# Fewer early weight sums beside the embedding, and the spread of the value differences from another engine's DMA queue

## The chip, the core and the metric

The kernel runs on one core of one Trainium2 chip. The metric is the device time of one execution in microseconds (us). The kernel before takes 813.34 us, the median of three runs (813.11 to 813.79).

## The reference

One layer of a small trunk, in float32, for 512 positions of width 2048. With depth 1 only the first mixer runs, sliding-window attention:

```
hn = rmsnorm(x, norm_g)
q, k, v, gate = split(hn @ swa_w_in)         # 32 query heads, 4 key/value heads, 64 wide
scores = q k^T / 8 + bias(distance), masked to a window of 128 back
probs  = softmax with a sink term in the denominator
y   = (probs v * silu(gate)) @ swa_w_out
x   = x + y
emb = p @ ple_proj                           # 512 x 256 @ 256 x 2048
g   = sigmoid(rmsnorm(x, ple_norm) @ ple_gate)
out = rmsnorm(x + emb * g, final_g)
```

## The kernel before

TensorE multiplies float32 as three products of a high and a low part (`mm3`, L129 to L134): ScalarE casts each block of weights to its high part (`whi`, L115), VectorE subtracts to get the low part (`wlo`, L116), and three matmuls of 512 columns follow. A block of weights is 128 x 1024 floats, 512 KB. `Weights` (L88) loads them through SyncE's queue (L105) into three raw buffers; a raw buffer is free again when the `wlo` of three blocks before is made.

The program has four stretches: the first products of q, k and v while x streams in (to about 71 us), the first gate block (71 to 81 us), the **embedding** `emb = p @ ple_proj` (`embed`, L903; 81.5 to 103.3 us on TensorE), and the attention loop (L944), in which TensorE's long projections (`proj`) are interleaved with 64 small attention blocks. After it come the output projection and the gate of the embedding, both as Strassen-like seven products of sub-blocks. Those need sums of blocks of weights (`w_out`, `ple_gate`), and the sums are prepared in DRAM long before: `sum_weights(i)` (L697) issues on even steps a copy of one block, DRAM to DRAM, from SyncE's queue (L700), and on odd steps, seven steps behind, an accumulating DMA onto that copy from GpSimd's queue (L702). There are 118 steps (`SUM_STEPS`), of which the first `SUMS_EARLY` belong to the embedding and the rest are spread evenly over the 64 attention blocks (`sums_in`, L932).

The embedding has 16 small steps (j = 0 to 3 over columns, t = 0 to 3 over rows), each with six matmuls into a bank of PSUM. For even t ScalarE copies the bank out (L914), for odd t VectorE does (L916), and GpSimd's queue then stores the pair to DRAM (`embedded`, L917). The copies go to a tile with three buffers (tag `u`), so the copy for one pair waits until the store of the third pair before it has landed. At t = 1 of each j the next block of weights is loaded, cast and subtracted (L919). Beside it run "chores" (L452): GpSimd builds differences of neighbouring value tiles (L441, L442), ScalarE and VectorE split them in high and low parts (L386, L387), and `spread_diff` (L446) copies them within SBUF to the places where the attention reads them (`DV`, first read by L595). That is four DMAs of 64 rows x 2 KB for each of three differences, twelve in all, and they are issued from SyncE's queue. In the order of the 16 steps (n = 4j + t) the three spreads come at n = 7, 9 and 11; the loads of weights come at n = 1, 5, 9 and 13, after the matmuls and ahead of the chores of the same step. The sums come last in a step.

Here the order of TensorE, SyncE, VectorE, ScalarE and GpSimd is the order of the program (`manual_schedule`, L351). Every engine runs its instructions in that order, and an instruction that waits holds up what stands behind it on its engine, DMA issues included.

The blocks of weights are numbered as they are loaded: 0 and 1 are the first gate block, 2 is `p` transposed, 3 to 6 are `ple_proj`, 7 and 8 the first block of q in the attention loop, 9 and 10 the second. "raw 8" below is the load of block 8, "whi 8" and "wlo 8" its parts.

Of the kernel before, what the change touches and what calls it, by code (L numbers as in the profile page):

```python
# [11 lines left out]
F32 = mybir.dt.float32  # L12
# [17 lines left out]
HB = P // 2  # L30
# [25 lines left out]
def trunk_kernel(ctx: ExitStack, tc: tile.TileContext, a: dict):  # L56
    nc = tc.nc
# [151 lines left out]
    for k in range(KC):  # L209
# [54 lines left out]
        else:  # L264
            high()
            if k == 1:
                src = xw[:, w_at[512] : w_at[512] + 256]
# [143 lines left out]
    for b in range(exact, BUCKETS):  # L411
        d = np.nonzero(bk == b)[0]
        if len(d):
            lo, n = P - 1 + int(d.min()), len(d)
# [16 lines left out]
    DV = apool.tile([P, NB - 1, 2, KVH * 2 * HD], F32R, name="DV")  # L431
# [14 lines left out]
    def spread_diff(n):  # L446
        src = diffs["all"][:, (n - 1) * S : n * S]
        for b in range(2):
            for o in range(2):
                nc.sync.dma_start(DV[HB * o : HB * o + HB, n - 1, b].bitcast(F32), src[HB * b : HB * b + HB])  # L450

    def first_chores(i, step):  # L452

        if step == 0 and i < NB - 1:
            make_diff(i + 1)
        if step and 1 <= i < NB:
            diffs[i][step - 1]()
        if step == 2 and 1 <= i - 1 < NB:
            spread_diff(i - 1)
        if step and 1 <= i - 2 < NB:  # L460
            split(V[i - 2], values[i - 2])[step - 1]()
# [230 lines left out]
                copies.append((t, block(nm, *first, jj, m) if first else summed[nm, {6: 7, 4: 6}[p], jj, m]))  # L692
                adds.append((t, block(nm, *{7: (2, 2), 5: (1, 2), 6: (1, 1), 4: (2, 1)}[p], jj, m)))
    SUM_STEPS = 2 * len(copies) + 6
    SUMS_EARLY = 16

    def sum_weights(i):  # L697

# [204 lines left out]
    def embed():  # L903

        h, l = (v.rearrange("p k c -> p (k c)").rearrange("p (k t) -> p k t", k=2) for v in W.get(2))
        for j in range(4):
            wh, wl = (v.rearrange("p k c -> p (k c)").rearrange("p (k c) -> p k c", k=2) for v in W.get(3 + j))
            for t in range(NB):
                e_ps = bank(f"e{t}_{j}", "to"[t % 2])
                for k in range(2):  # L910
                    mm3(e_ps, h[:, k, blk(t)], l[:, k, blk(t)], wh[:, k], wl[:, k], k == 0, k == 1)
                if t % 2 == 0:
                    both = apool.tile([P, 2, S], F32, tag="u", name=f"both{t}_{j}", bufs=3)
                    nc.scalar.copy(both[:, 0], e_ps)  # L914
                else:
                    nc.vector.tensor_copy(both[:, 1], e_ps)  # L916
                    nc.gpsimd.dma_start(embedded[t // 2, j], both.rearrange("p b c -> p (b c)"))  # L917
                if t == 1 and W.todo:
                    W.todo.pop(0)()  # L919
                for _ in range(2 if t == 3 else 1):  # L920
                    first_chores(*next(early_chores, (NB + 2, 0)))
                for n in early_sums.get(4 * j + t, ()):
                    sum_weights(n)
        for v in early_chores:
            first_chores(*v)

    early_chores = ((i, step) for i in range(NB + 2) for step in range(3))
    early_sums = {0: range(0, 4, 2), 2: range(4, 8, 2), 4: range(8, 12, 2), 6: range(12, 16, 2), 8: (7, 9), 11: (11, 13), 14: (15,)}
    embed()
    blocks = TWOS * UNITS  # L930

    def sums_in(i):  # L932

        n = SUM_STEPS - SUMS_EARLY
        return range(SUMS_EARLY + i * n // blocks, SUMS_EARLY + (i + 1) * n // blocks)

# [464 lines left out]
    n = done[3]  # L1401
# [87 lines left out]
```

## Time and profile before

| | |
|---|---|
| median of three runs | 813.34 us |
| profiled execution | 813.76 us |
| its span, first to last instruction | 812.1 us |
| TensorE busy | 786.7 us (97%) |
| VectorE busy | 585.3 us (72%) |
| ScalarE busy | 506.8 us (62%) |
| GpSimd busy | 148.7 us (18%) |
| moved by DMA | 191.52 MB, mean 236 GB/s |
| SyncE's DMA queue (q1, hardware) | 52.6% of 16 DMA engines' span |
| GpSimd's DMA queue (q0, software) | 28.1% |

PE is TensorE, PEld its weight loads, DVE is VectorE, ACT is ScalarE, POOL is GpSimd, SP is SyncE; SPq is SyncE's queue issuing a DMA. A row of the timeline has start, duration, engine, line, operation, tiles and count, and in brackets the idle time before it and what ended it. A row of waits has the total, the number and the longest. PEclk is the granted clock of TensorE as a share of full speed. "DMA share" is the mean busy share of the 16 DMA engines. Matmuls overlap, so their starts are counted here and not their durations.

### The profile page before, as it was taken

The numbers are of one execution on the slowest core, as the hardware profiler recorded it, in microseconds if no ns is written. First come the engines' busy times: TensorE is split into PE (matmuls) and PEld (weight loads), VectorE is DVE, ScalarE is ACT, GpSimd is POOL, SyncE is SP. The second block draws the span as 40 slices with busy tenths as digits, with TensorE's granted clock in tenths as the row PEclk, the third lists the DMA queues.
The fourth block names the chain that finished last, engine by engine and source line by source line (L and its number), as shares of the span: only waits on it lengthen the run. The fifth ranks groups of instructions, "written<-read, shape, count | busy, mean of one in ns | idle before, by whom it ended". The sixth has DMA issues, their size and how long they took to land.

```text
span 812.1 us, 11213 instructions
## 1 busy us (share of the span) xinstructions
PE 786.7 (97%) x3740; PEld 655.6 (81%) x3740; DVE 585.3 (72%) x1159; ACT 506.8 (62%) x1071; POOL 148.7 (18%) x256
## 2 busy tenths in 40 slices
PE   9999959999999999999999999999999999999993
PEld 8888838888888888888888888888888888888883
DVE  4555426877587767867676779977887675798986
ACT  6652425867576666766665665445668865666855
POOL 0200420323233141323233310000000012030100
PEclk9999979999999999999999999999999999999997
DMA  9976899988979897997889658876787399697743
GB/s 340 286 220 211 268 301 308 260 227 252 238 209 253 232 263 177 260 251 219 226 255 225 150 149 334 308 238 209 230 274 248 110 364 205 210 196 255 215 140 120
DMA packets 46282, 191.52 MB, mean 236 GB/s; under 512 B 6848, under 2 KB 7872, under 8 KB 41104
## 3 DMA queue, kind: packets, MB, share of 16 engines
q1 hardware_dynamic: 36992, 145.40, 52.6%
q0 software_dynamic: 9232, 45.41, 28.1%
q8 instruction: 29, 0.48, 0.2%
q14 instruction: 29, 0.24, 0.1%
HBM read 179.72 MB, written 67.16 MB: 304 GB/s over the span
## 4 chain that ended last, share of the span: by engine, by line
PE 81%; DVE 8%; DMA 5%; ACT 3%; issue 1%; SPq 1%; ACTq 0%; DVEq 0%
PE gps L132 6%; PE gps L133 6%; PE gps L134 6%; PE qps L132 6%; PE qps L133 6%; PE qps L134 6%; PE g L133 5%; PE g L134 5%; PE g L132 5%; PE o L133 5%; PE o L134 5%; PE o L132 5%; DMA wraw<-in_w_q 2%; DMA wraw<-in_w_gate_in 2%; PE s L487 2%; PE vps L300 2%
## 5 line engine op out<-in xcount | busy, mean ns | idle before, releaser
L743 ACT CAST bhi<-braw 128x1024 fp32r<-128x1024 f32 x94 | 98.8, 1052 | 69.3 <-PE o L134 22.9
L744 DVE TENSOR_TENSOR blo<-braw,bhi 128x1024 fp32r<-128x1024 f32 x94 | 114.4, 1222 | 37.5 <-ACT bhi L743 37.0
L132 PE MATMUL gps<-xh,whi 128*128 128x512 f32 x256 | 100.0, 391 | 0.0
L133 PE MATMUL gps<-xl,whi 128*128 128x512 f32 x256 | 99.9, 390 | 0.0
L134 PE MATMUL gps<-xh,wlo 128*128 128x512 f32 x256 | 99.8, 390 | 0.0
L132 PE MATMUL qps<-xh,whi 128*128 128x512 f32 x224 | 88.7, 396 | 7.4 <-ACT whi L115 7.4
L116 DVE TENSOR_TENSOR wlo<-wraw,whi 128x1024 fp32r<-128x1024 f32 x65 | 79.2, 1220 | 19.0 <-ACT whi L115 19.0
L134 PE MATMUL qps<-xh,wlo 128*128 128x512 f32 x224 | 88.1, 393 | 0.0
L133 PE MATMUL qps<-xl,whi 128*128 128x512 f32 x224 | 88.1, 393 | 0.0
L115 ACT CAST whi<-wraw 128x1024 fp32r<-128x1024 f32 x65 | 67.5, 1040 | 13.0 <-DMA wraw<-in_w_q 8.8
L133 PE MATMUL g<-blo,fhg 128*128 128x512 f32 x192 | 74.9, 390 | 0.5 <-DVE blo L744 0.5
L133 PE MATMUL o<-blo,fho 128*128 128x512 f32 x192 | 75.0, 390 | 0.2 <-DVE blo L744 0.2
L132 PE MATMUL g<-bhi,fhg 128*128 128x512 f32 x192 | 75.2, 392 | 0.0
L132 PE MATMUL o<-bhi,fho 128*128 128x512 f32 x192 | 74.8, 390 | 0.0
L134 PE MATMUL g<-bhi,flg 128*128 128x512 f32 x192 | 74.8, 390 | 0.0
L134 PE MATMUL o<-bhi,flo 128*128 128x512 f32 x192 | 74.8, 389 | 0.0
L567 POOL TENSOR_SCALAR_AFFINE_SELECT own<-r 64x512 fp32r<-64x512 f32 (+1 forms) x48 | 32.4, 675 | 228.9 <-DVE r L557 215.6
L557 DVE TENSOR_TENSOR r<-pt,r 128x256 fp32r<-128x256 f32 x64 | 27.1, 424 | 63.2 <-ACT r L556 62.3
L556 ACT CAST r<-pt 128x256 fp32r<-128x256 f32 x64 | 23.8, 372 | 73.8 <-PE pt L551 73.7
L502 POOL COPY t<-sinkb 128x2 f32<-128x2 f32 x64 | 50.6, 796 | 33.5 <-issue 33.5
L134 PEld LDWEIGHTS gps<-xh,wlo 128*128 128x128 f32 x256 | 48.1, 188 | 10.2
L132 PEld LDWEIGHTS gps<-xh,whi 128*128 128x128 f32 x256 | 48.1, 188 | 9.5 <-issue 0.4
(229 smaller groups left out, 1771.9 us busy)
## 6 DMA issues: line engine op xcount, KB each, us to landing
wraw<-in_w_gate_in SPq DMA_DIRECT2D x32, 512.0 KB, 6.8
w_out<-in_w_out POOLq DMA_DIRECT2D x32, 512.0 KB, 7.8
braw<-w_out SPq DMA_DIRECT2D x32, 512.0 KB, 5.1
wraw<-in_w_q SPq DMA_DIRECT2D x28, 512.0 KB, 6.3
braw<-in_ple_gate SPq DMA_DIRECT2D x24, 512.0 KB, 5.3
braw<-in_w_out SPq DMA_DIRECT2D x22, 512.0 KB, 4.3
xw<-in_first SPq DMA_DIRECT2D x14, 640.5 KB, 7.1
w_out<-in_w_out SPq DMA_DIRECT2D x16, 512.0 KB, 8.8
```

What stands on the lines that cost most here:

```text
L115: nc.scalar.copy(hi, raw)
L116: nc.vector.tensor_sub(lo, raw, hi.bitcast(F32))
L132: nc.tensor.matmul(ps, sh, mh, start=first, stop=False, skip_group_check=more)
L133: nc.tensor.matmul(ps, sh, ml, start=False, stop=False, skip_group_check=more)
L134: nc.tensor.matmul(ps, sl, mh, start=False, stop=last, skip_group_check=more)
L300: nc.tensor.matmul(v_ps[t], h[:, c], part_of(high_at, 256, 512), start=f, stop=e, skip_group_check=True)
L502: nc.gpsimd.tensor_copy(two(0, W + W - 1 if late else W, 1), sinkb[:, d : d + 1].unsqueeze(1).to_broadcast([P, 2, 1]))
L556: nc.scalar.copy(rh, src)
L557: nc.vector.tensor_sub(rl, src, rh.bitcast(F32))
L567: nc.gpsimd.affine_select(out=flat(own), in_=flat(r).bitcast(F32), pattern=[[0, 8], [sign, HB]], compare_op=ALU.is_ge, fill=0.0, base=-HB ...
L743: nc.scalar.copy(hi, raw)
L744: nc.vector.tensor_sub(lo, raw, hi.bitcast(F32))
```

## The change

Two things are changed in the embedding's stretch. The early sums are cut from 16 steps (eight copies from SyncE's queue, five accumulations from GpSimd's queue) to 7 steps (four copies, no accumulation); the steps left out go to the attention blocks, which now share 111 steps where they shared 102. The four copies stand at n = 1, 4, 7 and 10. And the twelve DMAs of `spread_diff` are issued from ScalarE's queue where they were issued from SyncE's.

```diff
@@ spread_diff @@
         src = diffs["all"][:, (n - 1) * S : n * S]
         for b in range(2):
             for o in range(2):
-                nc.sync.dma_start(DV[HB * o : HB * o + HB, n - 1, b].bitcast(F32), src[HB * b : HB * b + HB])
+                nc.scalar.dma_start(DV[HB * o : HB * o + HB, n - 1, b].bitcast(F32), src[HB * b : HB * b + HB])
@@ sums @@
     SUM_STEPS = 2 * len(copies) + 6
-    SUMS_EARLY = 16
+    SUMS_EARLY = 7
@@ order of the embedding's stretch @@
-    early_sums = {0: range(0, 4, 2), 2: range(4, 8, 2), 4: range(8, 12, 2), 6: range(12, 16, 2), 8: (7, 9), 11: (11, 13), 14: (15,)}
+    early_sums = {1: (0,), 4: (2,), 7: (4,), 10: (6,)}
```

## The prediction

> **What bounds the kernel now.** I read the busy times first, then a table of stretches, the waits of TensorE, and the chain of work that ended last. The busy times say that TensorE is the bound:
>
> ```profile
> PE 786.7 (97%) x3740; PEld 655.6 (81%) x3740; DVE 585.3 (72%) x1159; ACT 506.8 (62%) x1071; POOL 148.7 (18%) x256
> ```
>
> So only time can be won in which TensorE stands still or runs at a lower clock. The stretches around the embedding show where it does (last columns: granted clock, DMA share, GB/s):
>
> ```profile
> core 0: us, PE busy (x) PEld busy (x) DVE busy (x) ACT busy (x) POOL busy (x), PEclk, DMA share, GB/s
> 80.00:92.00 12.00, 12.00 (x55) 9.93 (x54) 4.96 (x7) 4.64 (x8) 3.37 (x6) 1.00 0.70 234
> 92.00:104.00 12.00, 12.00 (x56) 9.96 (x54) 6.85 (x11) 5.08 (x10) 7.68 (x11) 1.00 1.01 253
> 104.00:112.00 8.00, 5.53 (x25) 4.09 (x23) 1.29 (x7) 0.58 (x1) 0.85 (x4) 1.00 1.02 311
> 112.00:124.00 12.00, 4.58 (x11) 3.10 (x11) 3.54 (x10) 4.77 (x10) 2.10 (x8) 0.57 1.02 328
> ```
>
> TensorE is full until 104 us, idle for about 10 us after it, and at 0.57 of its clock from 112 to 124; the DMA engines are full from 92 us on. The waits between 70 and 150 us name the two holes and what stands behind the second:
>
> ```profile
> ACT both L914 <- DMA embedded<-both: 7.8, 2, 6.8
> PE qps L132 <- ACT whi L115: 7.4, 1, 7.4
> DVE both L916 <- DMA embedded<-both: 5.6, 1, 5.6
> PE s L487 <- DVE sm L520: 2.5, 1, 2.5
> ```
>
> The third loss is the clock after the long hole. The embedding's rows give the pace at full clock, TensorE's timeline the pace after the hole:
>
> ```profile
> L132 PE MATMUL e<-whi,whi x32: 389/389/389, 81.6 to 102.6; 128*128 128x512 f32 x32
> ...
> 119.49 0.80 PE L132 MATMUL qps<-xh,whi 128*128 128x512 f32 x1 [7.38 <-ACT whi L115]
> 123.88 0.39 PE L132 MATMUL qps<-xh,whi 128*128 128x512 f32 x1
> ```
>
> 31 triples of matmuls in 21.0 us are 0.227 us each. Between 119.49 and 123.88 start nine, in 4.39 us instead of 2.04: 2.35 us lost. Together 2.5 + 7.4 + 2.35 = 12.2 us, which is all that this change can reach. The chain says why the 7.4 us arise:
>
> ```profile
> 102.19 16.12 DMA wraw<-in_w_q
> ...
> 120.72 15.80 DMA wraw<-in_w_gate_in
> ```
>
> Raw 8 is issued at 102.19 us and takes 16.1 us to land. It is issued so late because of what stands before it on SyncE's queue:
>
> ```profile
> 88.28 3.54 SPq L450 DMA_DIRECT2D DV<-diffs  x4
> ...
> 93.69 8.47 SPq L450 DMA_DIRECT2D DV<-diffs  x8
> 102.19 1.17 SPq L105 DMA_DIRECT2D wraw<-in_w_q  x2
> ...
> 120.72 5.48 SPq L105 DMA_DIRECT2D wraw<-in_w_gate_in  x2
> 126.25 0.49 SPq L700 DMA_DIRECT2D small<-in_w_out  x1
> 126.80 1.96 SPq L469 DMA_DIRECT2D bias<-tdram  x4
> 130.12 0.35 SPq L105 DMA_DIRECT2D wraw<-in_w_q  x1
> 136.54 0.49 SPq L700 DMA_DIRECT2D small<-in_w_out  x1
> ```
>
> The last five rows show a rule of this program that matters below: the copy at 136.54 needs no data of anyone, yet starts when the load issued at 120.72 has landed (120.72 + 15.80 = 136.52), and that load stands eight hardware transfers ahead of it (2 + 1 + 4 + 1). A transfer waits for the eighth one before it.
>
> **The change part by part.** *Five accumulations leave the stretch.* The DMA answers for 81 to 92 us (before the accumulations) and 92 to 104 us (with them), last column the median us to landing:
>
> ```profile
> embedded<-both POOLq DMA_DIRECT2D x3, 512.0 KB, 4.4
> DV<-diffs SPq DMA_DIRECT2D x4, 128.0 KB, 4.4
> wraw<-in_w_q SPq DMA_DIRECT2D x1, 512.0 KB, 7.1
> ...
> q0 software_dynamic: 404, 1.82, 65.3%
> embedded<-both POOLq DMA_DIRECT2D x4, 512.0 KB, 12.3
> DV<-diffs SPq DMA_DIRECT2D x8, 128.0 KB, 10.9
> ```
>
> From 92 us GpSimd's queue holds 65% of the engines, and everything lands two to three times later. The attention loop gives the price of one accumulation and the cover for moving it there:
>
> ```profile
> q0 software_dynamic: 3801, 24.85, 41.4%
> ...
> 150.00:480.00 330.00, 329.92 (x1630) 277.30 (x1629) 239.46 (x662) 221.50 (x611) 101.84 (x170) 1.00 0.86 228
> DMA to landing us min/median/max: 3.6/6.2/8.6
> ```
>
> 24.85 MB are 47 accumulations of 0.524 MB in 0.414 x 330 = 137 us of all engines: 2.9 us each. Five are 14.5 us of DMA work taken out of the time from 94 to about 128 us. So I expect landings there like those of 81 to 92 us. The 2.5 us hole goes: the last VectorE copy waited 5.6 us for a store that took over 12 us and held up the softmax (L520) behind it; the store in question is that of three pairs, or 36 matmuls and 8.2 us, before, so with 4.4 us it has landed before the copy's own matmuls end.
>
> *Four copies leave, and nine steps go into the loop.* The copies ran from 66 to 87 us beside a full TensorE, so their going wins nothing. In the loop the nine transfers cost at most 9 x 2.9 = 26 us of engines over 330 us, so the share goes from 0.86 to at most 0.94. What hides them: raw loads landed there in 8.6 us at most (third row), and TensorE was busy for 329.92 of 330 us. I take 0; if that cover were gone, each us by which a block comes too late is a us of TensorE.
>
> *Twelve DMAs move to ScalarE's queue.* On SyncE this frees raw 8: the spreads no longer stand ahead of it. But the rule of eight still ties it to them if, as I assume, both hardware queues count together: eight ahead of raw 8 now stands the second transfer of the second spread, issued by ScalarE. (If they count apart, raw 8 goes out some 10 us earlier and is hidden anyway.) On ScalarE each issue occupies the engine, and behind it stand the copies L914 and the casts `whi`. The price of one issue on ScalarE is shown nowhere; SyncE's rows for the same transfers bound it:
>
> ```profile
> L450 SPq DMA_DIRECT2D DV<-diffs x12: 461/629/1746, 88.3 to 101.5; - x12
> ```
>
> Twelve are 12 x 0.46 = 5.5 us at the least and 12 x 1.75 = 21.0 at the most. I take the group of four at 88.28 us, issued with no accumulation in flight, as the later ones now will be: 3.54 us, three times, 10.6 us. How much of that ScalarE has to spare is in its timeline (idle time in brackets), with the two readers of block 7:
>
> ```profile
> 94.03 0.59 ACT L914 COPY both<-e 128x512 f32<-128x512 f32 x1 [1.83 <-PE e L134]
> 97.14 0.59 ACT L914 COPY both<-e 128x512 f32<-128x512 f32 x1 [0.96 <-DMA embedded<-both]
> 100.79 0.59 ACT L914 COPY both<-e 128x512 f32<-128x512 f32 x1 [2.76 <-PE e L134]
> 101.27 1.05 ACT L115 CAST whi<-wraw 128x1024 fp32r<-128x1024 f32 x1
> 102.36 1.23 DVE L116 TENSOR_TENSOR wlo<-wraw,whi 128x1024 fp32r<-128x1024 f32 x1 [0.85 <-ACT whi L115]
> 104.00 0.39 PE L134 MATMUL qps<-xh,wlo 128*128 128x512 f32 x1
> ```
>
> All three spreads fall between 92.2 us and whi 7 at 101.27. ScalarE is idle there for 1.83 + 0.96 + 2.76 = 5.55 us; wlo 7 is done at 103.59 and first read at 104.00, 0.4 us to spare. So 6.0 us are hidden and 10.6 - 6.0 = 4.6 us are not: whi 7 and wlo 7 come 4.6 us later, and TensorE waits for them ahead of the first block of q (some 1 us of it already in the embedding, where whi 6 slips by 3.54 - 1.83 = 1.7 us). By the bounds the new wait is 0 to 15.0 us.
>
> The Trainium skill speaks against weighing this at all: "DMA: Bandwidth & Descriptors", section "Issuing engines are not separate DMA queues", says that DMAs of all queues share the same 16 engines and that issuing from another engine saves only the issue time, usually small beside the DMA itself. By that the new wait would be 0, the second outcome below. The row differs: 3.54 us of issue beside landings of 4.4.
>
> *Raw 8 then.* ScalarE starts the first spread at 92.2, is done at 95.7, needs 2.2 us for a copy, two short casts and whi 6 (durations 0.59, 0.41, 0.41 and 1.05, overlapping a little), and issues the transfer that raw 8 waits for at 98.5. It lands 4.4 us later, raw 8 another 7.1: 110.0; whi 8 and wlo 8 take 2.3: 112.3. Without holes TensorE would want block 8 at 119.49 - 7.4 - 2.5 = 109.6, with the new wait at 114.2. It is hidden, with 1.9 us to spare.
>
> **Sum.** 12.2 us won, 4.6 lost: 7.6 us. The profiled execution took 813.76 us, so 806.2; the median of the runs is 0.42 below it: **805.7 us**.
>
> On the clock, the Trainium skill, "TensorE: Matmul & The Clock Gate", section "What's actually happening", says that one idle window of about 3.4 us halves it. The trace agrees with the 7.4 us hole (0.57), and the 2.5 us one cost no clock. By that rule the rest of the new wait, 3.6 us in one piece, could cost up to 2.35 us more: 808.1, inside the range.
>
> **The rivals.**
>
> *Short issues.* ScalarE's own queue is empty, so its issues take the least that SyncE's did, 5.5 us in all, inside the 6.0. For it: half of SyncE's twelve took 0.63 us or less. Then raw 8 becomes the next limit: its forerunner issues at 96.7, so 96.7 + 4.4 + 7.1 = 108.2 and both parts at 110.5, where wlo 8 is wanted at 110.1. 12.2 - 0.4 = 11.8 us: 801.5.
>
> *Long issues.* ScalarE's issues all last like a long one of SyncE's in the chain:
>
> ```profile
> 94.89 1.64 SPq L450
> ```
>
> At 1.6 us each, 19.2 - 6.0 = 13.2 us are lost: 1.0 us slower, 814.3. It decides from 1.5 us each (18.2 us in all). Against it: a group without accumulations took 3.54.
>
> *The rule of eight keeps raw 8 late (slower).* The engines stay full without the accumulations, too: eight stores, three raw loads and the spreads remain. With the landings of 92 to 104 us the forerunner lands at 98.5 + 10.9 = 109.4 and only then raw 8 is issued, to land 16.1 later at 125.5. The long hole ended 1.2 us after raw 8's landing at 118.3, now at 126.7 instead of 119.5: 7.2 us slower, 820.5. It decides where the two landings together exceed 118.3 - 98.5 = 19.8 us; I count 11.5. Against it: 14.5 us of work are gone from the engines.
>
> *The loop.* If the loop's DMA cannot take nine more steps, the gain is eaten later; with a share of at most 0.94 I see no price to give, and count it with small gains.
>
> **How the numbers follow.** The forecast 0.52; short issues 0.33; a smaller gain (4 us down to 0.2%) 0.02; long issues 0.06, of which 0.04 ends within 0.2%; raw 8 late 0.07. 0.2% is 1.6 us, about what a measurement of this kernel tells from no change. Faster 0.52 + 0.33 + 0.02 = 0.87, same 0.04, slower 0.02 + 0.07 = 0.09. The range goes from 801.0, under the short issues and the ceiling of 12.2 us (801.1), to 810.0, where the issues cost 1.24 us each (14.9 - 6.0 = 8.9 us lost); the two slower cases lie outside.
>
> **What would show each step.** GpSimd's queue well under 65% of the engines from 92 to 104 us, stores landing in 4 to 7 us, no wait of L487. Twelve L450 rows on ScalarE's queue whose sum is 10.6; whi 7 at 105.9 instead of 101.27, and a wait of TensorE before the first q for L115 or L116. Raw 8 issued at about 103, right after a spread lands, and no 7 us hole in the middle of that block. TensorE full in the loop, at a DMA share under 0.95. The forecast is wrong if the issues on ScalarE sum to under 6 or over 15 us, or if a raw load is late again.

## The result and the profile after

The changed kernel takes 803.1 us (median of four runs, 802.7 to 804.6), the kernel before beside it 813.6 us (four runs, 813.1 to 814.6). The ratio is 0.987, with an interval of 0.986 to 0.989: 10.5 us faster, where 7.6 us were forecast. The profiled execution took 802.72 us with a span of 801.0, against 813.76 and 812.1 before.

The table of stretches of the changed kernel, with the columns of the one in the prediction:

```profile
core 0: us, PE busy (x) PEld busy (x) DVE busy (x) ACT busy (x) POOL busy (x), PEclk, DMA share, GB/s
92.00:104.00 12.00, 11.46 (x51) 8.95 (x50) 5.24 (x9) 3.62 (x9) 3.00 (x5) 1.00 0.99 341
104.00:112.00 8.00, 6.89 (x31) 5.31 (x30) 5.85 (x16) 6.22 (x13) 4.49 (x11) 1.00 0.99 338
112.00:124.00 12.00, 12.00 (x58) 9.99 (x57) 7.00 (x24) 7.76 (x20) 0.55 (x3) 1.00 1.03 299
...
150.00:480.00 330.00, 330.00 (x1630) 277.50 (x1630) 240.79 (x652) 221.35 (x607) 107.47 (x169) 1.00 0.87 236
```

TensorE is full again from 112 us on, at full clock, and in the loop. What is missing lies between 92 and 112 us, 0.54 + 1.11 us. All of TensorE's waits between 70 and 150 us:

```profile
PE qps L132 <- ACT whi L115: 0.6, 1, 0.6
PE e L133 <- DVE wlo L116: 0.5, 1, 0.5
PE qps L134 <- DVE wlo L116: 0.5, 1, 0.5
```

Both old holes are gone, and with them the slow clock. In their place stand three small waits, all for a block of weights that ScalarE casts late. ScalarE's timeline in the changed kernel shows why it is late:

```profile
91.45 0.59 ACT L914 COPY both<-e 128x512 f32<-128x512 f32 x1 [1.23 <-PE e L134]
91.50 0.50 ACTq L450 DMA_DIRECT2D DV<-diffs  x1
...
92.04 3.34 ACTq L450 DMA_DIRECT2D DV<-diffs  x3
95.48 0.59 ACT L914 COPY both<-e 128x512 f32<-128x512 f32 x1 [3.14 <-PE e L134]
95.63 1.12 ACTq L450 DMA_DIRECT2D DV<-diffs  x1
...
96.57 1.05 ACT L115 CAST whi<-wraw 128x1024 fp32r<-128x1024 f32 x1
96.79 4.05 ACTq L450 DMA_DIRECT2D DV<-diffs  x3
100.94 0.59 ACT L914 COPY both<-e 128x512 f32<-128x512 f32 x1 [3.32 <-PE e L134]
101.07 0.47 ACTq L450 DMA_DIRECT2D DV<-diffs  x1
...
101.57 2.08 ACTq L450 DMA_DIRECT2D DV<-diffs  x3
103.75 0.59 ACT L914 COPY both<-e 128x512 f32<-128x512 f32 x1 [1.92 <-PE e L134]
104.24 1.05 ACT L115 CAST whi<-wraw 128x1024 fp32r<-128x1024 f32 x1
```

An issue keeps back what stands behind it: each later L914 row starts 0.1 us after the issues ahead of it end. The brackets name TensorE, but the time is the issue's. An issue itself does not wait for the compute ahead of it: the one at 91.50 runs beside the copy of 91.45, those at 95.63 and 96.79 beside a copy and whi 6. The last row is whi 7; it stood at 101.27 before.

The DMA answer for 92 to 104 us in the changed kernel (queue with packets, MB and share of 16 engines, then median us to landing):

```profile
q0 software_dynamic: 575, 2.10, 46.6%
...
embedded<-both POOLq DMA_DIRECT2D x3, 512.0 KB, 8.0
...
wraw<-in_w_q SPq DMA_DIRECT2D x2, 512.0 KB, 6.7
```

The engines are as full as before (0.99), but they move 341 GB/s instead of 253, and a raw load lands in 6.7 us instead of 16.1.

### The profile page after: what moved, and what is told of

Same layout as the page of the kernel before. It is cut to its first block, busy times and chain, and to the rows that moved or that the text cites. A ratio compares the mean times of both kernels' runs of the same rounds, so it can differ in the third digit from the quotient of the medians.

```text
span 801.0 us, 11208 instructions
## 1 busy us (share of the span) xinstructions
PE 784.4 (98%) x3740; PEld 654.5 (82%) x3740; DVE 585.1 (73%) x1159; ACT 506.7 (63%) x1071; POOL 154.3 (19%) x256
## 4 chain that ended last, share of the span: by engine, by line
PE 88%; DVE 6%; ACT 2%; DMA 2%; issue 1%; ACTq 1%; DVEq 0%
PE qps L132 7%; PE qps L134 7%; PE qps L133 7%; PE gps L133 7%; PE gps L132 7%; PE gps L134 7%; PE g L133 5%; PE g L134 5%; PE g L132 5%; PE o L133 5%; PE o L134 5%; PE o L132 5%; PE s L487 2%; PE vps L300 2%; PE o L593 2%; PE pt L551 2%
## 5 line engine op out<-in xcount | busy, mean ns | idle before, releaser
L116 DVE TENSOR_TENSOR wlo<-wraw,whi 128x1024 fp32r<-128x1024 f32 x65 | 79.2, 1220 | 10.6 <-ACT whi L115 10.6
L502 POOL COPY t<-sinkb 128x2 f32<-128x2 f32 x64 | 57.3, 905 | 26.3 <-issue 21.0
L718 POOL DMA_DIRECT2D grown<-in_ple_gate x16 | 13.8, 861 | 227.7 <-DVE blo L744 222.5
```

The costliest lines, as they stand in the source:

```text
L116: nc.vector.tensor_sub(lo, raw, hi.bitcast(F32))
L502: nc.gpsimd.tensor_copy(two(0, W + W - 1 if late else W, 1), sinkb[:, d : d + 1].unsqueeze(1).to_broadcast([P, 2, 1]))
```

## The experiments

Each ratio is to the kernel before, measured beside it on the same chip; its median was 814.05, 813.72 and 813.86 us beside the first four, the next four and the last two of the runs below.

**The sums alone.** From the changed kernel:

```diff
-                nc.scalar.dma_start(DV[...].bitcast(F32), src[...])
+                nc.sync.dma_start(DV[...].bitcast(F32), src[...])
```

> Only the sums are changed (four early copies, no early accumulation); the spreads stay on SyncE's queue. If the accumulations made the transfers land late, raw 8 is still issued near 101 us, behind the spreads, but lands some 7 us later and block 8 is ready about when TensorE wants it: 801.5 to 803, as fast as the whole change or faster, since ScalarE issues nothing. Rival, the place of raw 8 on SyncE's queue was the cause: it is as late as before, the hole of 7 us stays, 809 to 812.

Measured: 808.6 us, ratio 0.9945 (0.9919 to 0.9970), the median of ten runs from 806.5 to 817.1, the widest spread of all; it lies between the expectation and its rival. SyncE's queue, and TensorE's longest wait:

```profile
94.07 4.63 SPq L450 DMA_DIRECT2D DV<-diffs  x4
...
100.22 4.71 SPq L450 DMA_DIRECT2D DV<-diffs  x4
104.97 2.62 SPq L105 DMA_DIRECT2D wraw<-in_w_q  x2
```

```profile
PE qps L132 <- ACT whi L115: 4.0, 1, 4.0
```

The chain of waits has the landing of that load:

```profile
104.97 7.96 DMA wraw<-in_w_q
```

Raw 8 still stands behind the spreads, goes out at 104.97, and now lands in 8 us. That shortens the long hole from 7.4 to 4.0 us and leaves it there. So the accumulations are the cause of the slow landing, and the order on SyncE's queue the cause of the late start. The four copies that left are not: with all eight back and no accumulation (further below) raw 8 lands in 6.4 us.

**The spread alone.** The kernel before, with `nc.scalar` in the same line; the accumulations stay.

> Only the spreads are moved to ScalarE's queue; the early sums stay as before, five accumulations included. If the accumulations were the cause, the stores still land after 12 us, the softmax of the first block still waits 2.5 us or more, ScalarE's issues get longer than 11.4 us in sum and the engine loses 4 us or more: 806 to 813. Rival, raw 8's place was the cause: raw 8 goes out near 92 us, the long hole is gone, 802 to 805.

Measured: 808.8 us, 0.9936 (0.9921 to 0.9951). From the chain of waits, with TensorE's wait behind it:

```profile
95.98 11.16 DMA DV<-diffs
107.16 0.47 ACTq L450
```

```profile
PE qps L132 <- ACT whi L115: 4.8, 1, 4.8
```

With the accumulations in flight a spread takes 11.2 us to land, and the twelfth issue waits for the landing of the sixth. Behind it stand a copy and whi 7. Each half of the change by itself wins about 5 us and leaves one hole of 4 to 5 us. The two gains, 5.5 and 5.3 us, add up to about that of the whole change.

**Twice as many issues.** From the changed kernel, each DMA of the spread cut in two:

```diff
+                for c in range(2):
+                    cs = slice(c * 256, (c + 1) * 256)
+                    nc.scalar.dma_start(DV[..., n - 1, b, cs].bitcast(F32), src[..., cs])
-                nc.scalar.dma_start(DV[..., n - 1, b].bitcast(F32), src[...])
```

> The changed kernel with each spread of four transfers cut into eight of half the columns: the same bytes, 24 issues on ScalarE's queue instead of 12. If an issue's time goes with the instruction and what exceeds the hidden 8.5 us is paid by TensorE in full, the sum of the issues goes from 11.4 to about 18 to 23 us and the time by 7 to 11 us: 810 to 814. Rival, the issue time goes with the bytes, or is hidden: within 1 us of 803.

Measured: 811.3 us, 0.9970 (0.9958 to 0.9982). The group of issues (least, median and longest ns), and TensorE's two longest waits:

```profile
L452 ACTq DMA_DIRECT2D DV<-diffs x24: 468/607/1591, 91.4 to 109.8; - x24
...
DMA to landing us min/median/max: 2.0/3.2/6.0
```

```profile
PE qps L132 <- ACT whi L115: 2.8, 1, 2.8
PE e L132 <- ACT whi L115: 2.7, 1, 2.7
```

The same bytes in 24 pieces land twice as fast, yet the issues keep ScalarE for 18.4 us (its rows summed) instead of 11.6, and the time rises by about 8 us. More issues for the same bytes are what costs, not the transfers. But 1.9 us of the 18.4 are two waits in which an issue stands until a load from SyncE's queue has landed. The chain of waits has the longer one:

```profile
101.96 4.74 DMA wraw<-in_w_q
...
106.72 0.47 ACTq L452
```

The issue ahead of the one at 106.72 ended at 105.50.

**The spread behind raw 8 on SyncE.** The sums as changed; the spreads are issued from SyncE at n = 13, 14 and 15, behind the load of raw 8:

```diff
-            spread_diff(i - 1)
+            spreads.append(i - 1)
...
+                if 4 * j + t in (13, 14, 15):
+                    spread_diff(spreads.pop(0))
```

> The sums as in the changed kernel; the spreads on SyncE's queue again, but behind the load of the last early block (at the steps n = 13, 14 and 15). Neither ScalarE nor the loads wait for them. If the 2.5 us that TensorE still loses are ScalarE's issues, they go: 800 to 801.5. Rival, they come from the load on the DMA engines: no difference to the changed kernel, 803.

Measured: 801.2 us, 0.9843 (0.9829 to 0.9858), about 2 us better than the changed kernel. SyncE's queue and the one wait of TensorE:

```profile
92.50 0.35 SPq L105 DMA_DIRECT2D wraw<-in_w_q  x1
92.89 12.05 SPq L450 DMA_DIRECT2D DV<-diffs  x12
```

```profile
PE qps L134 <- DVE wlo L116: 0.3, 1, 0.3
```

Twelve issues take 12 us on SyncE as well. There nothing urgent stands behind them.

**The same late spread from ScalarE.** The kernel just shown with `nc.scalar`.

> The changed kernel with the twelve issues on ScalarE's queue put behind the cast of block 7 (steps n = 13, 14 and 15); behind them stands the cast of block 8. If an issue costs what stands behind it on its engine, whi 7 comes in time and whi 8 late: some 11 us of issues from 102.4 us on, block 8 about 6 us after TensorE wants it, 806 to 808. Rival, the early places were the harm: 801 to 802, as from SyncE's queue.

Measured: 808.0 us, 0.9931 (0.9916 to 0.9945). ScalarE's timeline:

```profile
104.82 8.95 ACTq L450 DMA_DIRECT2D DV<-diffs  x8
113.82 1.04 ACT L115 CAST whi<-wraw 128x1024 fp32r<-128x1024 f32 x1 [8.43 <-DMA DV<-diffs]
```

Here the long row of issues stands right ahead of a cast that TensorE needs, and TensorE waits 5.3 us for it. Some 1.9 us of the row, from 109.40 to 111.27, are again a wait for a load that SyncE issued:

```profile
103.59 7.68 DMA wraw<-in_w_q
...
111.36 0.47 ACTq L450
```

The same transfers at the same place in the program come out 6.7 us apart by the engine that issues them: behind SyncE's row stood nothing urgent, behind ScalarE's a cast.

**The spread from GpSimd.** The changed kernel with `nc.gpsimd` in the line of the spread, at the old places.

> The changed kernel with the spreads issued from GpSimd's queue at their places in the program; behind them stand the stores of the embedding. GpSimd has time: 3 us busy of 12. If one of its issues takes about 0.6 us as the stores' do, a store comes up to 2.5 us later, within the slack of three buffers, and TensorE loses little: 801 to 803. Rival, the stores land late and the copies wait: 804 to 807.

Measured: 801.3 us, 0.9848 (0.9831 to 0.9864). Its issues:

```profile
L450 POOL DMA_DIRECT2D DV<-diffs x12: 522/526/551, 94.7 to 104.3; - x12
...
DMA to landing us min/median/max: 4.5/6.2/9.5
```

An issue takes 0.53 us there, nearly constant, and TensorE has no wait left between 70 and 160 us, so nothing that it needs soon stood behind them. This kernel and the late spread from SyncE beat both the changed kernel and the one before.

**The changed kernel once more**, measured with the two kernels above and the next.

> The changed kernel as it is, beside the next three on the same chip: 10 us below the kernel before, 803 to 804.

Measured: 802.9 us, 0.9868 (0.9853 to 0.9882).

**The early copies.** First the eight copies at their old places with the accumulations put off to the first blocks of the loop:

```diff
-    SUMS_EARLY = 7
+    SUMS_EARLY = 16
...
-    early_sums = {1: (0,), 4: (2,), 7: (4,), 10: (6,)}
+    early_sums = {0: range(0, 4, 2), 2: range(4, 8, 2), 4: range(8, 12, 2), 6: range(12, 16, 2)}
+    put_off = [7, 9, 11, 13, 15]
...
+            if i % 2 == 0 and put_off:
+                sum_weights(put_off.pop(0))
```

> The changed kernel with the eight copies again at their old places in the embedding, while the five accumulations are put off into the first blocks of the attention loop. If the copies were hidden beside a full TensorE, the time is that of the changed kernel within 1 us. Rival, the copies' traffic was part of the late landings: 2 us or more above it.

Measured: 806.1 us, 0.9906 (0.9891 to 0.9920), 3.1 us worse than the changed kernel beside it. To see whether the copies did that, they were put back by themselves, with the loop's other steps in the changed kernel's order:

```diff
-    early_sums = {1: (0,), 4: (2,), 7: (4,), 10: (6,)}
+    early_sums = {0: range(0, 4, 2), 2: range(4, 8, 2), 4: range(8, 12, 2), 6: range(12, 16, 2)}
...
             for n in sums_in(i):
-                sum_weights(n)
+                if n not in range(8, 16, 2):
+                    sum_weights(n)
```

> The changed kernel with all eight early copies back at their old places (steps n = 0, 2, 4 and 6 of the embedding); the five accumulations stay in the attention loop, where the order of the other steps is that of the changed kernel and the four copies already made are left out. So it differs from the changed kernel by the copies alone. Theory A, copies beside a full TensorE are free, and the run with early copies and put-off accumulations lost its 3 us to a loop copy that was issued at 98.75 us beside the spreads: 803 us, TensorE's waits before the first q at most 1.2 us as in the changed kernel. Theory B, the copies' backlog in the DMA engines delays the first spread's landings and so the last issues on ScalarE's queue: 806 us as in that run, the last issue waiting at about 103 us and a wait of TensorE of some 3 us for whi 7.

And with no early sums at all (`SUMS_EARLY = 0`, `early_sums = {}`):

> The changed kernel with no early sums at all: the four copies too go into the loop, which then shares all 118 steps. Theory A (copies are free beside a full TensorE): 803 us, as with four copies. Theory B (each copy in the stretch costs, some 0.7 us of the 3 us between four and eight): 800 us, no wait of TensorE before the first q. Under both the loop's DMA share stays under 0.90 and TensorE full in it.

Measured: 806.1 us for eight copies (0.9894, 0.9865 to 0.9922), one of its four runs at 801.7; 807.2 us for none (0.9918, 0.9900 to 0.9936). Neither theory holds: more copies cost 3 us, and fewer cost 4. In their traces, one of each, the four kernels come in the order of the moment at which ScalarE is through with its twelve issues (first column: start and duration of the last rows of issues):

| | issues end | whi 7 | TensorE waits before or at the first q | median us |
|---|---|---|---|---|
| changed kernel (four copies) | 103.7 | 104.24 | 0.5 + 0.6 + 0.5 | 803.1 |
| eight copies | 104.9 | 105.45 | 2.3 + 0.5 | 806.1 |
| eight copies, sums put off | 105.5 | 106.05 | 3.1 + 0.5 | 806.1 |
| no copies | 105.8 | 106.35 | 3.4 + 0.5 | 807.2 |

1.2 us on ScalarE between the first two rows became 3 us. TensorE's timeline with eight copies shows the rest:

```profile
106.55 0.50 PE L132 MATMUL qps<-xh,whi 128*128 128x512 f32 x1 [2.29 <-ACT whi L115]
...
107.81 0.79 PE L134 MATMUL qps<-xh,wlo 128*128 128x512 f32 x1 [0.54 <-DVE wlo L116]
...
110.95 0.39 PE L132 MATMUL qps<-xh,whi 128*128 128x512 f32 x1
```

From 107.81 to 110.95 start seven matmuls, in 3.14 us instead of 1.6 (0.23 each): 1.5 us of slow clock, on top of 1.2 us more of waiting. Executions of one kernel differ, too: in the trace of the changed kernel once more the issues end at 104.7, 1.0 us later, of which 0.6 is a later start of the embedding; TensorE's waits are 0.2 + 1.2 + 0.5, and the clock stays up (803.8 us in that execution). And with eight copies one run of four took 801.7.

Why the issues end sooner with four copies is not settled. In all four kernels of the table the seventh issue goes out when raw 8 has landed (issued at 91.9 to 92.1 us, landed 5.7 to 6.5 us later). The difference arises behind it: from the seventh issue's start to the twelfth's end pass 5.3 us in the changed kernel and 6.5 to 7.9 us in the others. The last row of issues without copies:

```profile
101.69 4.08 ACTq L450 DMA_DIRECT2D DV<-diffs  x3
```

Three issues take 4.1 us there and 2.1 in the changed kernel; what lengthens them was not tried. It was not tried whether other places for four copies would do the same.

## Why the prediction was right, and where it was not

*What could be won, 12.2 us.* Held. Both holes and the slow clock went. The attention's first read of `DV` (L595) starts at 133.0 us instead of 143.3. It is 10.3 us earlier, of 11.1 in the span. 12.2 less the new loss of 2.6 is 9.6. Matmul by matmul, the changed kernel is 9.8 us ahead where the slow clock of the kernel before ended (123.88 there, 114.08 here), 10.3 at the first L595 and 10.8 from the matmul of 160.8 us on. Two short waits of L595 in the kernel before, 0.6 us in all for a tile that ScalarE writes late (`own`, L577), are most of the last 1.0 us; the changed kernel does not have them. The forecast had no term for them.

*Five accumulations out make landings like those of 81 to 92 us.* Held for the raw loads (6.7 us; 7.1 forecast), less so for the stores: 8.0 us in the median where 4.4 was taken. No copy waited for them, so it cost nothing. GpSimd's queue came down to 46.6% from 65.3%.

*The copies' going wins nothing.* Fell. Beside the changed kernel, more copies and fewer both cost 3 to 4 us, and the end of ScalarE's issues moves with them. The cover I named, a full TensorE beside the copies, is there; what I did not weigh is the queue of issues behind them, some 25 us later. That the change keeps four copies, and not eight or none, was worth those 3 to 4 us for no reason that I had: so much of the 10.5 us is luck, and with eight or none the time would have been 806 to 807, beside the 805.7 forecast.

*The loop takes nine more steps for nothing.* Held: 330.00 of 330 us busy at a DMA share of 0.87, under the 0.94 allowed.

*Twelve issues on ScalarE, 10.6 us, 6.0 hidden, 4.6 lost.* This is the term that was mis-sized. The issues came to 11.6 us (the timeline's rows: 0.50 + 3.34 + 1.12 + 4.05 + 0.47 + 2.08), close to the 10.6. But whi 7 came 3.0 us late instead of 4.6, and the first block's low part was read at 106.60 instead of 104.00, 2.6 us late:

```profile
106.60 0.50 PE L134 MATMUL qps<-xh,wlo 128*128 128x512 f32 x1 [0.54 <-DVE wlo L116]
```

ScalarE's idle time ahead of the three copies is 3.14 + 3.32 + 1.92 = 8.4 us, where it was 5.55: 2.8 us more, which is the delay of whi 7. The other 11.6 - 8.4 = 3.2 us of issue lay beside compute. I let every issue stand alone on the engine; in fact ScalarE goes on with copies and casts that were handed to it before the issue. The Trainium skill, "Advanced Engine Details and Errata", section "Sequencer Loop", says that engine instructions are pushed into a queue, and that others can be read and queued while a control instruction runs. The first half agrees with these 3.2 us. The second half is not what the rows show for a DMA issue: the copy at 95.48 starts 0.10 us after the issues end, though with eight copies, where they ended at 94.65, it ran at 94.74.

The new wait also came in pieces of 0.5 to 0.6 us, so it cost no clock; the forecast had left 2.35 us for that inside its range.

*Raw 8 by the rule of eight.* The rule held, with both hardware queues in one count; the place that I gave raw 8 in it did not. I put raw 8 behind the second transfer of the second spread, and so at 103 us. It went out at once when its buffer was free, ahead of every transfer of the second spread (95.63), and the chain of waits leads from its landing to ScalarE's seventh issue:

```profile
91.90 6.39 DMA wraw<-in_w_q
...
98.31 1.89 ACTq L450
```

That issue and that load share no data. Here the issue ahead of it had ended at 98.26, so the tie cost nothing; the rows of 106.72 (twice as many issues) and 111.36 (the late spread from ScalarE) show the same tie with waits of 1.2 and 1.9 us. The traces also record the semaphore, the counter on which a transfer reports its landing: the transfers of SyncE's and ScalarE's queues take the same eight in turn, and an issue waits until the transfer that had its semaphore before has landed. In that turn raw 8 stands ahead of the first spread, so no spread keeps it back, and the eighth transfer behind it is the seventh of the spreads. Why it has that place, when the spread stands earlier in the program, no run shows. So the parenthesis came true, by which raw 8 goes out some 10 us earlier and is hidden anyway, but not its condition that the queues count apart; and the slower rival had no ground, since raw 8 was tied to no spread. In the spread alone, the twelfth issue's wait for the sixth is the same rule: five spreads, a load and a copy from SyncE stand between them.

*Short issues (801.5 us).* Fell by its price: the least issue was 0.47 us, but the sum was 11.6 and not 5.5. Its time is nearly that of the two kernels in which ScalarE issues nothing (801.2 and 801.3), since both mean a new wait of about zero. *Long issues* fell too: 11.6 us is under the 18.2 from which it decided; with 24 issues, at 18.4 us with their waits, the gain all but went (0.997).

*Issue time beside the DMA.* The sentence was taken from "DMA: Bandwidth & Descriptors", section "Issuing engines are not separate DMA queues", in the Trainium skill: issuing from another engine saves only the issue time, usually small beside the DMA. Here each of the twelve transfers takes 1.0 us to issue in the mean and 6.4 in the median to land. The issue is the smaller part, but it is the part that the engine pays, and moving it off ScalarE was worth about 2 us.

## What to carry to other kernels

A DMA's issue is work of the engine that issues it. Count the issues, about 1 us each for these transfers from ScalarE or SyncE, and look at which instructions stand behind them on that engine and who waits for those; put them on the queue where nothing urgent stands behind, or behind the urgent load on the same queue. The queues of two engines need not be independent: here an issue on one waited for the landing of a load on the other. A load that lands late can have two causes, a late start behind other issues and a slow flight beside other traffic; each taken away alone won half and left a hole. And where a wait of about 2 us ends in a slow clock, a cause of 1 us can cost 3, as with eight copies.

## What the runs showed of the hardware that I had not expected

An issue of the same 128 KB within SBUF took 0.47 to 1.89 us on ScalarE in the changed kernel (rows of 11.6 for twelve) and about as long on SyncE (12.05), but a nearly constant 0.53 us on GpSimd; on ScalarE cutting the pieces in two brought the median only from 0.77 to 0.61 us.

An issue on ScalarE runs beside compute that was handed on before it (3.2 of 11.6 us), and holds back all compute behind it (the copies start 0.1 us after it ends).

The transfers of ScalarE's and SyncE's queues are tied to each other eight apart: issues on ScalarE started 0.02 and 0.09 us after the landing of a load from SyncE (106.70 and 106.72, 111.27 and 111.36). The wait stands in the program's own instructions, so this is how the program was built and not shown to be the chip's.

A hole of 2.29 us and one of 0.54, which ended 1.3 us after the first, brought the clock down with eight copies (0.43 us a matmul instead of 0.23), while the single hole of 2.5 us before the change did not (granted clock 1.00 from 104 to 112 us). The Trainium skill, "TensorE: Matmul & The Clock Gate", section "What's actually happening", has a free-running window of about 3.4 us that must be idle. From the end of the score matmuls behind the embedding (L487, 104.26) to 107.81 lie about 3.6 us in which only two matmuls ran; whether a window with so few counts as idle no run here tested.
